# Filler weights of a scan: the low parts made by a ScalarE copy and an accumulating DMA

## Chip, core and metric

The kernel runs on one core of a Trainium2 chip. The metric is device time in microseconds of one execution, the median of several. The engines are named as in the profile: PE is TensorE's matmul and PEld its weight load, DVE is VectorE, ACT is ScalarE, POOL is GpSimd, SP is SyncE, which issues most of the DMAs.

## The reference, cut to what matters

One layer of a bidirectional encoder over 1024 positions and 1024 channels, all in float32:

```python
def _token_mixers(h, w_in, dw_w, dw_b, ln_w, ln_b, pw_w, lb, norm_w, o_w):
    proj = jnp.einsum("bsd,de->bse", h, w_in)
    glu_in, q, v, z_f, z_b, og, g_a, g_b = jnp.split(proj, SPLIT_POINTS, axis=-1)
    a = jax.nn.glu(glu_in, axis=-1)
    a = _dwconv_centred(a, dw_w, dw_b)
    a = jax.nn.silu(_layernorm(a, ln_w, ln_b))
    a = jnp.einsum("bsc,cd->bsd", a, pw_w)
    o = _bi_hgrn2(q, v, z_f, z_b, lb[0], lb[1])
    of = o * lax.rsqrt(jnp.mean(o * o, axis=-1, keepdims=True) + EPS)
    of = of.reshape(o.shape[0], o.shape[1], HGRN_WIDTH) * norm_w.astype(jnp.float32)
    bmix = (of * jax.nn.silu(og.astype(jnp.float32))).astype(h.dtype)
    bmix = jnp.einsum("bse,ed->bsd", bmix, o_w)
    return jax.nn.sigmoid(g_a) * a + jax.nn.sigmoid(g_b) * bmix
```

`_bi_hgrn2` is a chunkwise gated scan over 8 heads of 128 channels, once forward and once backward. After the mixers come an output projection with a residual, a gated feed-forward network and a final norm.

## The kernel before, in words

**Split products.** A float32 product is made of three matmuls of a faster 4-byte type (float32r). Each operand is split into a high part `hi`, a copy in that type, and a low part `lo`, the operand less `hi`. `mm3` (L142 to L149) issues, for one 128x128 block of weights, `hi` times the activation's high part (L147), `hi` times its low part (L148) and `lo` times its high part (L149). `split` (L122, its instructions on L123) makes the two parts: ACT copies, and DVE (or POOL) subtracts.

**Weight tiles.** A projection of 128 output channels over all positions is one job of `std_job` (L249). Its `prep` loads 128 columns of the weights (512 KB) into a raw page (tile `wr`, two buffers, L132, loaded by SP on L134) and splits it into two pages (tile `wp`, four buffers, L137). Its `run` goes through two halves of the positions with eight blocks each, 48 matmuls in all, and yields after every two blocks (a piece of six matmuls). `run_jobs` (L193) prepares the next job when a job starts, so that a tile's pages become free when the tile two before it is done. `Stream.fill(n)` runs n pieces.

**The stages.** The kernel first normalises the input, then projects, convolves, and goes on to the scan stage, which is about L1016 to L1417. Of the 56 column tiles for q, v, the gates and the forget gates, 34 are made as pairs in earlier stages. The other 22 (`rest`) are kept for the scan stage as filler: their stream is called `dense`. Twenty of them are one job each. The last two are one job (`duo_job`, L267) that alternates between two tiles.

**The scan stage.** There are 8 heads with two halves of 512 positions. For each half, `scan_inputs` (L1053) loads q and the forget gates (tile `zi`) and makes f and k on ACT, `scan_base` (L1077) prepares the factors `qF`, `kG`, `Qh`, `Kh` and `DE` on DVE (most through `tt`, L1042), and `scan_levels` (L1137) goes through four levels. In each, PE makes small matmuls (L1162, L1174, L1188) from qF and kG, and DVE then scales qF and kG for the next level. `scan_states` (L1238, PE on L1245 and L1254) and `scan_outputs` (L1277, PE on L1295, ACT on L1297, L1300 and L1314, POOL's `ors` on L509 and L510) follow. Between these steps `between` puts FILL = 1.3 pieces of `dense` on PE, and two steps of the next half's base on DVE. Ahead of the first head stand 21 pieces:

```python
    cur = Base(scan_inputs(0))
    ins = scan_inputs(1)
    dense.fill(21)
```

The order of PE's instructions is written out by hand (the order of the program). On the other engines a planner orders the instructions by a model of their times and by their place in the program, save those pinned to it.

**Accumulating DMAs.** Elsewhere in the kernel, sums of weight tiles are made by a DMA that POOL issues and that adds a tile in DRAM to a tile in SBUF (`G.dma_start(o, a, accum_op=ALU.add)`, L300, tile `sw` from `in_w_in_dram`). None is in the scan stage.

Of the kernel before, what the change touches and what calls it, by code (L numbers as in the profile page):

```python
# [10 lines left out]
F32 = mybir.dt.float32  # L11
# [3 lines left out]
AF = mybir.ActivationFunctionType  # L15
ALU = mybir.AluOpType
# [30 lines left out]
def tile_hybrid_encoder(  # L47
# [24 lines left out]
    V, A, G, T = nc.vector, nc.scalar, nc.gpsimd, nc.tensor  # L72

    S, D = x.shape[1], x.shape[2]
    ND = D // P
# [17 lines left out]
    def nm(s):  # L93
        uid[0] += 1
        return f"{s}_{uid[0]}"
# [3 lines left out]
    def bank(tag):  # L99
        return ps.tile([P, H], F32, tag=tag, name=nm(tag), bufs=BANKS[tag])  # L100

    def page(pool, tag, bufs, dt=F32):
        return pool.tile([P, H], dt, tag=tag, name=nm(tag), bufs=bufs)
# [18 lines left out]
    def split(hi, lo, src, eng, late=False):  # L122
        parts = A.copy(hi, src), eng.tensor_tensor(lo, src, hi.bitcast(F32), op=ALU.subtract)  # L123
        if late:
            for i in parts:
                pin(i)
        return hi, lo

    def w_cols(w, r0, nk, c0, cols=P):
        return w[0, r0 : r0 + nk * P, c0 : c0 + cols].rearrange("(k p) e -> p k e", p=P)  # L130

    def raw_w(src, nk):  # L132
        t = mp.tile([P, nk, P], F32, tag="wr", name=nm("wr"), bufs=2)
        nc.sync.dma_start(t, src)  # L134
        return t

    def w_page(nk, pool=None):  # L137
        if pool is None:
            return mp.tile([P, nk, P], F32R, tag="wp", name=nm("wp"), bufs=4)
        return pool.tile([P, nk, P], F32R, tag="wq", name=nm("wq"), bufs=3)  # L140

    def mm3(acc, w, act, k, first, last, again=False):  # L142


        whi, wlo = w
        ahi, alo = act
        T.matmul(acc, whi[:, k, :], ahi, start=first, stop=False, skip_group_check=again)  # L147
        T.matmul(acc, whi[:, k, :], alo, start=False, stop=False, skip_group_check=again)  # L148
        T.matmul(acc, wlo[:, k, :], ahi, start=False, stop=last, skip_group_check=again)  # L149
# [99 lines left out]
    def std_job(src, nk, acts, evac, halves=(0, 1), step=2):  # L249


        def prep():
            raw = raw_w(src, nk)
            return split(w_page(nk), w_page(nk), raw, V)

        def run(w, halves=halves):
            for half in halves:
                acc = bank("mm")
                for k in range(nk):
                    mm3(acc, w, acts(k, half), k, k == 0, k == nk - 1)  # L260
                    if k % step == step - 1 or k == nk - 1:
                        yield
                evac(half, acc)

        return prep, run

    def duo_job(src0, src1, nk, acts, evac0, evac1):  # L267

        both = [std_job(src0, nk, acts, evac0), std_job(src1, nk, acts, evac1)]

        def prep():
            return [p() for p, _ in both]

        def run(w):
            for half in range(2):
                for (_, r), wi in zip(both, w):
                    yield from r(wi, (half,))

        return prep, run
# [219 lines left out]
    def in_cols(c0):  # L499
        return w_cols(w_in, 0, ND, c0)  # L500
# [278 lines left out]
    def glu_tiles(j, halves):  # L779
        yield std_job(in_cols(CW + j * P), ND, h_std, evac_b(j), halves)  # L780
        yield std_job(in_cols(j * P), ND, h_std, evac_a(j), halves)
# [191 lines left out]
    for half in range(2):  # L973
# [27 lines left out]
        at = 0  # L1001
# [12 lines left out]


    rest = todo[2 * NPAIRS :]  # L1016
    rest_jobs = [std_job(in_cols(c), ND, h_std, e) for c, e in rest[:-2]]
    (c0, e0), (c1, e1) = rest[-2:]
    rest_jobs.append(duo_job(in_cols(c0), in_cols(c1), ND, h_std, e0, e1))

# [564 lines left out]
    def fetch(src):  # L1585
        t = page(fu, "ft", 8)
        nc.sync.dma_start(t, src)
        return t
# [211 lines left out]
```

## Time and profile before

| | us |
|---|---|
| Median of three runs | 1792.36 |
| Lowest and highest run | 1791.06, 1793.42 |
| Span of the profiled execution, first to last instruction | 1788.8 |
| PE busy in that span | 1733.0 |
| DVE busy | 1250.4 |
| ACT busy | 775.0 |
| POOL busy | 153.8 |

The profiled execution's own time is known as its span; the runs' times, which take in what lies around the span, were measured apart from it. A row of a group has the line, the engine, the operation, the tiles (output, then inputs), the shapes and the count; behind the bar are the busy time, the mean duration in ns and the idle time of the engine ahead of it with who ended it. A row in the order of time has its start, its length, and in brackets the idle time ahead of it with who ended that. A wait has who waited for whom, the total in us, the number of waits and the longest.

### The profile page before, as it was taken

How to read it: one execution, taken by the hardware profiler on the slowest of the kernel's cores; microseconds unless marked ns; L12 is line 12 of the kernel's file. 1: busy time of each engine (PE TensorE's matmuls, PEld its weight loads, DVE VectorE, ACT ScalarE, POOL GpSimd, SP SyncE). 2: the span in 40 equal slices, each digit the busy share in tenths (PEclk: the TensorE clock that was granted, in tenths of full speed). 3: DMA queues.
4: the chain of work that ended last, by engine and by line, in shares of the span. 5: the costliest groups of instructions: out<-in, count | busy, mean ns of one | idle time of the engine just before them, and what ended most of it. 6: DMA issues, size and time to landing. Idle time of an engine off the chain costs nothing.

```text
span 1788.8 us, 27583 instructions
## 1 busy us (share of the span) xinstructions
PE 1733.0 (97%) x10632; PEld 1416.7 (79%) x10638; DVE 1250.4 (70%) x1884; ACT 775.0 (43%) x1490; POOL 153.8 (9%) x168
## 2 busy tenths in 40 slices
PE   8989999999999999999999999999999999999997
PEld 6878877888777777777778888878888888888885
DVE  5599999746569999999645557667667667544455
ACT  7344333334555566655442245344344344422123
POOL 2201111000000000000000002011111111000000
PEclk9999999999999999999999999999999999999999
DMA  8657887743663433333257665567667665534233
GB/s 285 216 151 187 185 185 185 199 150 126 199 214 101 125 119 119 119 119 101 90 180 219 200 201 177 153 142 159 151 144 158 142 151 133 161 103 126 79 91 135
DMA packets 317705, 276.41 MB, mean 155 GB/s; under 512 B 14462, under 2 KB 242566, under 8 KB 317574
## 3 DMA queue, kind: packets, MB, share of 16 engines
q1 hardware_dynamic: 276406, 242.15, 43.1%
q0 software_dynamic: 41168, 32.51, 12.6%
q8 instruction: 83, 1.36, 0.3%
q14 instruction: 48, 0.39, 0.1%
HBM read 185.73 MB, written 72.61 MB: 144 GB/s over the span
## 4 chain that ended last, share of the span: by engine, by line
PE 65%; DVE 19%; DMA 5%; issue 4%; ACT 4%; POOL 1%; SPq 0%; POOLq 0%; DVEq 0%; ACTq 0%
PE mm L147 16%; PE mm L148 16%; PE mm L149 16%; PE sc L147 3%; PE sc L149 3%; PE sc L148 3%; DVE acc L955 2%; DVE kG L1042 2%; DVE DE L1042 2%; DVE qF L1042 2%; DVE wp L123 2%; PE tr L147 1%; PE tr L149 1%; PE tr L148 1%; DVE DE L1098 1%
## 5 line engine op out<-in xcount | busy, mean ns | idle before, releaser
L147 PE MATMUL mm<-hx,wp 128*128 128x512 f32 x1128 | 454.8, 403 | 9.8 <-DVE ev L717 4.3
L149 PE MATMUL mm<-hx,wp 128*128 128x512 f32 x1128 | 441.7, 392 | 1.9 <-DVE wp L123 1.9
L148 PE MATMUL mm<-hx,wp 128*128 128x512 f32 x1128 | 441.4, 391 | 0.0
L123 ACT CAST wp<-wr 128x1024 fp32r<-128x1024 f32 (+2 forms) x179 | 167.0, 934 | 359.6 <-PE mm L148 271.5
L147 PEld LDWEIGHTS mm<-hx,wp 128*128 128x128 f32 x1128 | 212.5, 188 | 55.7 <-DVE ev L717 6.7
L123 DVE TENSOR_TENSOR wp<-wr,wp 128x1024 fp32r<-128x1024 f32 (+2 forms) x177 | 191.4, 1082 | 90.4 <-ACT wp L123 90.1
L149 PEld LDWEIGHTS mm<-hx,wp 128*128 128x128 f32 x1128 | 212.6, 188 | 49.3 <-DVE wp L123 3.2
L148 PEld LDWEIGHTS mm<-hx,wp 128*128 128x128 f32 x1128 | 212.9, 189 | 40.4 <-issue 0.2
L955 DVE SCALAR_TENSOR_TENSOR acc<-gl,v_b,acc 128x1024 f32<-128x1024 f32 x120 | 149.0, 1277 | 0.5
L1651 DVE TENSOR_TENSOR xr<-mm,xr 128x512 f32<-128x512 f32 x48 | 33.2, 691 | 73.1 <-PE mm L149 73.1
L367 ACT COPY su<-mm 128x512 f32<-128x512 f32 x78 | 45.2, 579 | 62.5 <-PE mm L149 61.5
L123 ACT CAST wq<-sw 128x1024 fp32r<-128x1024 f32 x39 | 41.0, 1051 | 64.4 <-issue 28.6
L1500 DVE SCALAR_TENSOR_TENSOR tm<-gp,v_a,tm 128x512 f32<-128x512 f32 x88 | 65.9, 749 | 2.0
L147 PE MATMUL mm<-hy,wp 128*128 128x512 f32 x156 | 61.5, 394 | 1.4 <-ACT su L367 1.4
L148 PE MATMUL mm<-hy,wp 128*128 128x512 f32 x156 | 61.1, 392 | 0.0
L147 PE MATMUL sc<-hy,wq 128*128 128x512 f32 x156 | 61.1, 392 | 0.0
L149 PE MATMUL sc<-hy,wq 128*128 128x512 f32 x156 | 61.1, 391 | 0.0
L147 PE MATMUL tr<-hx,wp 128*128 128x512 f32 x156 | 60.8, 390 | 0.0
L149 PE MATMUL tr<-hx,wp 128*128 128x512 f32 x156 | 60.7, 389 | 0.0
L148 PE MATMUL tr<-hx,wp 128*128 128x512 f32 x156 | 60.7, 389 | 0.0
L148 PE MATMUL sc<-hy,wq 128*128 128x512 f32 x156 | 60.7, 389 | 0.0
L149 PE MATMUL mm<-hy,wp 128*128 128x512 f32 x156 | 60.6, 389 | 0.0
(368 smaller groups left out, 3467.6 us busy)
## 6 DMA issues: line engine op xcount, KB each, us to landing
wr<-in_w_in_dram SPq DMA_DIRECT2D x56, 512.0 KB, 4.7
wr<-in_ffn_w_up_dram SPq DMA_DIRECT2D x24, 512.0 KB, 4.9
sw<-in_ffn_w_up_dram SPq DMA_DIRECT2D x44, 256.0 KB, 3.0
d_g<-ft SPq DMA_DIRECT2D x44, 256.0 KB, 2.7
sw<-in_ffn_w_up_dram POOLq DMA_DIRECT2D x20, 512.0 KB, 8.3
sw<-in_w_in_dram SPq DMA_DIRECT2D x34, 256.0 KB, 3.2
d_z<-ev SPq DMA_DIRECT2D x32, 256.0 KB, 3.1
zi<-d_z SPq DMA_DIRECT2D x32, 256.0 KB, 3.2
```

The source lines that it names most:

```text
L123: parts = A.copy(hi, src), eng.tensor_tensor(lo, src, hi.bitcast(F32), op=ALU.subtract)
L147: T.matmul(acc, whi[:, k, :], ahi, start=first, stop=False, skip_group_check=again)
L148: T.matmul(acc, whi[:, k, :], alo, start=False, stop=False, skip_group_check=again)
L149: T.matmul(acc, wlo[:, k, :], ahi, start=False, stop=last, skip_group_check=again)
L367: A.copy(t, acc)
L955: V.scalar_tensor_tensor(acc, g[:, k : k + S], tap(k), acc, op0=ALU.mult, op1=ALU.add)
L1042: V.tensor_tensor(o, a, b, op=op)
L1098: V.reciprocal(ed(D, 7), ed(0, D + 7))
L1500: V.scalar_tensor_tensor(c, g[:, o + k : o + k + H], vec("fdw", k * NF + j), c, op0=ALU.mult, op1=ALU.add,)
L1651: V.tensor_tensor(xr[i][half], acc, xr[i][half], op=ALU.add)
```

## The change

For twenty of the twenty-two filler tiles (all but the closing pair) the low part is made in another way. ACT still copies the raw page into `hi`. Then ACT, not DVE, writes minus `hi` into `lo`, and POOL issues a DMA that adds the weights in DRAM to `lo`, a second read of the same 512 KB. The raw page is then read by ACT alone. Besides, each job's `prep` asks for the raw page of the job after it, before its own copies; `fetch` remembers pages by their place in the weights.

```diff
+    def dma_job(src, nk, acts, evac, fetch, after):
+        def prep():
+            raw = fetch(src)
+            if after is not None:
+                fetch(after)
+            hi, lo = w_page(nk), w_page(nk)
+            A.copy(hi, raw)
+            A.activation(lo, hi.bitcast(F32), AF.Copy, scale=-1.0)
+            G.dma_start(lo, src, accum_op=ALU.add)
+            return hi, lo
+
+        return prep, std_job(None, nk, acts, evac)[1]
...
     rest = todo[2 * NPAIRS :]
-    rest_jobs = [std_job(in_cols(c), ND, h_std, e) for c, e in rest[:-2]]
+    fetched = {}
+
+    def fetch(src):
+        at = src.offset
+        if at not in fetched:
+            fetched[at] = raw_w(src, ND)
+        return fetched[at]
+
+    srcs = [in_cols(c) for c, _ in rest[:-2]]
+    rest_jobs = [
+        dma_job(src, ND, h_std, e, fetch, after)
+        for src, (_, e), after in zip(srcs, rest, srcs[1:] + [None])
+    ]
     (c0, e0), (c1, e1) = rest[-2:]
     rest_jobs.append(duo_job(in_cols(c0), in_cols(c1), ND, h_std, e0, e1))
```

## The prediction

> **What bounds the kernel now.** I read the page first, then the busy time by stretch, the waits and the chain of the stretch that the change touches, and last the order of time around the first filler tiles.
>
> ```profile
> span 1788.8 us, 27583 instructions
> PE 1733.0 (97%) x10632; PEld 1416.7 (79%) x10638; DVE 1250.4 (70%) x1884; ACT 775.0 (43%) x1490; POOL 153.8 (9%) x168
> ```
>
> TensorE bounds the whole. The edit works only in the scan stage, whose matmul tiles fill TensorE between the scan's steps, so the stretch table matters more.
>
> ```profile
> 495.00:520.00 25.00, 25.00 (x111) 20.59 (x110) 11.92 (x19) 15.38 (x23) 1.31 (x4) 1.00 0.81 255
> 525.00:866.00 341.00, 322.71 (x4210) 263.90 (x4215) 316.85 (x645) 197.67 (x482) 11.88 (x12) 1.00 0.35 111
> ```
>
> The columns are start:end, length, then the busy time of PE, PEld, DVE, ACT and POOL, the granted clock, the DMA share and GB/s. At the entry, 495 to 520, PE is busy in all 25.00 us and DVE in 11.92: PE alone sets the time there. In the body, 525 to 866, DVE is busy in 316.85 of 341 us (93%), PE has 18.3 us idle, ACT stands at 58%, and the clock is full.
>
> ```profile
> PE ob L1162 <- DVE qF L1042: 6.0, 7, 1.5
> PE tr L1245 <- DVE kG L1042: 4.7, 6, 1.8
> PE sc L1188 <- DVE qF L1042: 3.2, 6, 1.2
> PE ob L1295 <- DVE D L1230: 1.1, 1, 1.1
> PE ob L1162 <- ACT wp L123: 0.9, 1, 0.9
> DVE f L1074 <- ACT f L1067: 9.8, 4, 4.0
> DVE wp L123 <- ACT wp L123: 7.7, 4, 3.3
> ```
>
> These waits of the body (total us, times, longest) say whom PE waits for: DVE, 6.0 + 4.7 + 3.2 + 1.1 = 15.0 us in twenty waits. One of them in the order of time:
>
> ```profile
> 597.97 1.21 DVE L123 TENSOR_TENSOR wp<-wr,wp 128x1024 fp32r<-128x1024 f32 x1
> 599.10 0.68 DVE L1042 TENSOR_TENSOR qF<-qF,tb 128x512 f32<-128x512 f32 x1
> 599.93 0.46 PE L1162 MATMUL ob<-qF,A 128*32 128x32 f32 x32 [0.92 <-DVE qF L1042]
> ```
>
> The low part of a filler tile (L123, 1.21 us) stands on DVE ahead of the scan's qF, and PE idles 0.92 us for that qF. This is the place where the change can win.
>
> **What the body gains.** The chain of work of 525 to 866:
>
> ```profile
> by line: DVE kG L1042 11.1%; DVE qF L1042 10.1%; DVE DE L1042 9.7%; DVE wp L123 4.7%; DVE DE L1098 4.6%; DVE Kh L1045 4.6%; DVE Qh L1042 4.1%; issue 4.0%; DVE Sb L1347 3.0%; ACT tm L1314 2.7%; ACT jk L1300 2.5%; DVE Sf L1262 2.2%; ACT f L10
> 526.04 1.13 DVE wp L123
> 864.46 1.14 DVE wp L123
> ```
>
> DVE wp is 4.7% of 341 us, 16.0 us: fourteen steps of some 1.14 us, of which the first and the last stand here. The change takes twenty of the twenty-two low parts off DVE; the closing pair of tiles keeps its own. The step at 864.46 belongs to the pair and stays. The one at 526.04 lies before PE has reached the scan's first level, so its removal frees nothing on PE. Twelve steps are left: 12 x 1.14 = 13.7 us. The bound from above is what PE waits for DVE, 15.0. The bound from below is zero, if DVE then waits elsewhere as long (the f and wp rows: 9.8 + 7.7 us of DVE idle are no DVE work at all). I take 13.7, nearer to the upper end, because those twelve steps lie on the chain, not merely on a busy engine. What is late next is PE itself, at 95% of the body.
>
> **What ACT and the queues pay.**
>
> ```profile
> L123 ACT CAST wp<-wr 128x1024 fp32r<-128x1024 f32 x21 | 21.9, 1044 | 15.0 <-PE mm L148 12.8 <-DMA wr<-in_w_in_dram 2.1
> L123 DVE TENSOR_TENSOR wp<-wr,wp 128x1024 fp32r<-128x1024 f32 x21 | 25.7, 1222 | 12.7 <-ACT wp L123 12.7
> L300 POOL DMA_DIRECT2D sw<-in_w_in_dram x11: 1570/1579/1764, 122.5 to 316.7; - x11
> POOL ors L509 <- ACT jk L1300: 354.9, 7, 87.2
> q0 software_dynamic: 41168, 32.51, 12.6%
> ```
>
> The scaled copy reads and writes 1024 columns as the cast does, so I price it at the cast's 1.044 us: 20 x 1.044 = 20.9 us more on ACT against 20 x 1.222 = 24.4 us less on DVE. ACT's own steps on the chain (tm 2.7% and jk 2.5% in the row above, a further one cut off by the row's end) are some 7%, and 7% of 20.9 is 1.5 us. From below it is zero, where ACT idles behind the cast; from above three times the 0.9 us that PE already waits for an ACT cast, 2.7 us. I take 1.5. Queued behind the new copy on ACT are the scan's A, f, kT and tm, and it is for these that DVE and PE wait.
>
> POOL gets 20 issues of 1.579 us, 31.6 us in a stretch with 11.88 us of work. In the body only the ors pairs stand in its queue (seven, long idle before them); an ors caught behind an issue waits up to 1.6 us for it. The issues fill 9% of the stretch, so of seven ors 0.6 would be caught, for half an issue each: 0.5 us at most on the chain, and zero in the sum. What is new on POOL is that it waits for ACT's copy: behind that wait stand the next ors, and behind them ACT's tm. The accumulating traffic is 20 x 0.524 = 10.5 MB; at the q0 row's rate (12.6% of 1788.8 us for 32.51 MB) that is 73 us of all sixteen engines, and lifts the body's share from 0.35 to 0.56. I cost it at nothing, since the scan's own loads are issued far ahead of their use, as this pair of rows shows for zi (15.7 us from issue to first use):
>
> ```profile
> 612.16 2.07 SPq L1063 DMA_DIRECT2D zi<-d_z  x2
> 627.82 0.63 ACT L1064 ACTIVATE k<-zi 128x512 f32<-128x512 f32 x1
> ```
>
> Without that cover each load that meets a new transfer would be late by that transfer's share of the engines, 73 / 20 = 3.6 us.
>
> The raw loads issued two tiles ahead change nothing:
>
> ```profile
> 559.36 0.38 SPq L134 DMA_DIRECT2D wr<-in_w_in_dram  x1
> 596.32 1.04 ACT L123 CAST wp<-wr 128x1024 fp32r<-128x1024 f32 x1
> ```
>
> SP issues this tile's load 37 us before its cast already now, so the wait that an earlier issue could take away isn't there. On SP's queue the load moves ahead of a few stores and zi loads, at 0.38 us of issue each: zero, from both sides, as long as zi keeps its 15.7 us.
>
> **What the entry loses.** The new low part is hi, then the negative copy, then POOL's issue, then the landing, and the third product of the first tile needs it.
>
> ```profile
> 497.75 1.05 ACT L123 CAST wp<-wr 128x1024 fp32r<-128x1024 f32 x1 [1.68 <-PE mm L148]
> 498.84 1.22 DVE L123 TENSOR_TENSOR wp<-wr,wp 128x1024 fp32r<-128x1024 f32 x1 [2.52 <-ACT wp L123]
> 500.58 0.39 PE L147 MATMUL mm<-hx,wp 128*128 128x512 f32 x1
> 501.03 0.40 PE L149 MATMUL mm<-hx,wp 128*128 128x512 f32 x1
> sw<-in_w_in_dram POOLq DMA_DIRECT2D x11, 512.0 KB, 8.8
> DMA to landing us min/median/max: 3.2/4.2/10.7
> wr<-in_w_in_dram SPq DMA_DIRECT2D x21, 512.0 KB, 4.6
> 501.27 0.21 POOL L1037 MEMSET dg<- 128x128 f32 x1
> 529.25 0.73 PE L1174 MATMUL sc<-Qh,Kh 128*32 128x32 f32 x62
> ```
>
> The cast waits for a page that PE frees at about 497.7 (its releaser is PE), so it can't start earlier. It ends at 498.80, the negative copy at 499.84, and the accumulating DMA lands T later. The eleven accumulating loads of the same 512 KB from the same tensor land in 8.8 us (issue time included), so T = 8.8: 508.64. PE wants it at 501.03 (L149), and its order is fixed by hand: **a stall of 7.6 us**, where PE has been without a gap. PE reaches the scan's first level (L1174, 529.25) by working through the filler, so that the level moves by the whole stall. In general T - 1.2. The bounds for T: 4.6, the plain load of the same size, and 10.7, the longest landing of that line; if POOL's memsets (the last at 501.27) come first, 1.6 more.
>
> The second tile has its pages at 500.7 and a whole tile of time. The third must wait until the first is done:
>
> ```profile
> 511.25 0.39 PE L149 MATMUL mm<-hx,wp 128*128 128x512 f32 x1
> 522.81 0.39 PE L149 MATMUL mm<-hx,wp 128*128 128x512 f32 x1
> 524.42 1.04 ACT L123 CAST wp<-wr 128x1024 fp32r<-128x1024 f32 x1
> 539.81 0.39 PE L149 MATMUL mm<-hx,wp 128*128 128x512 f32 x1
> ```
>
> The first tile ends at 511.64; plus cast, copy and T that is 511.64 + 1.05 + 1.04 + 8.8 = 522.5 against a need at 522.81, both pushed by the same stall: no loss at 8.8, T - 9.1 above that. From the fourth on there are 15.4 us from cast to need (524.42 to 539.81, the shortest of the body) against 2.1 + T = 10.9, so the landing is hidden; it would show from T = 13.3.
>
> **The sum**, against this execution: -13.7 + 1.5 + 7.6 = -4.6 us on the span of 1788.8. The three runs' median, 1792.36, lies 3.6 above the span and within 0.1% of its fellows; I carry the difference over: 1792.36 - 4.6 = **1787.8**.
>
> By the Trainium skill, page "DMA: Bandwidth & Descriptors", section "Anatomy of one DMA — SWDGE (gpsimd) path", a GpSimd-issued DMA costs about 2.0 us plus bytes / 436 GB/s: 3.2 us for 512 KB, an estimate. With it the stall is 2.0 and the sum -10.2, 1782.2. The trace speaks against it for an accumulating transfer: 8.8.
>
> **Rivals.** About 0.2%, 3.6 us, is what a measurement of this kernel tells from no change.
>
> Slower: the landing at the entry. The entry is the stretch with a DMA share of 0.81, two accumulating transfers overlap there, and no DMA of the trace writes into an fp32r tile, so T may be longer than anything shown. Both the first and the third tile pay: (T - 1.2) + (T - 9.1) - 12.2. That is nothing at T = 11.2, 3.6 slower from T = 13.0, and 7.5 slower at 15: 1799.9. Against it: the eleven transfers behind the 8.8 and 10.7 ran in a stretch as busy as this one.
>
> ```profile
> 200.00:300.00 100.00, 98.94 (x434) 80.95 (x433) 97.22 (x93) 37.29 (x54) 16.66 (x15) 1.00 0.81 185
> ```
>
> There the share was 0.81 too. Chance 0.18.
>
> No change: DVE's saving turns into DVE idling. A run of DVE begins when ACT delivers f (9.8 us in four waits), and ACT gets the extra copy; the waits of DVE for a cast (7.7 us) show that a low part sometimes stood where DVE had nothing else. If half the twelve steps pay, -6.9 + 1.5 + 7.6 = +2.2: 1794.6. From 5.5 to 12.7 us of gain it is within 3.6. Chance 0.22, with 0.06 more for T between 11 and 13 with the full gain. Below 5.5 it is slower: 0.11.
>
> Faster by more: the accumulate lands like a plain load, T = 4.6, the stall is 3.4 and the sum -8.8: 1783.6. For it: both move the same 512 KB in 512-byte rows. Against it: the 8.8 row. Chance 0.05, the page's rule included.
>
> **How the numbers follow.** The forecast itself has 0.38. Faster: 0.38 + 0.05 = 0.43. Same: 0.22 + 0.06 = 0.28. Slower: 0.18 + 0.11 = 0.29. The range runs from the upper bound of the gain with the short landing, -15.0 + 3.4 + 1.5 = -10.1, rounded out to 1781, to the long landing of 15 us, 1800. The forecast's own range, T from 7 to 10.7 and the gain from 12.7 to 15.0, is 1785 to 1791.
>
> **What would show it.** Right: the low part's DVE rows are down to the closing pair in the scan; twenty ACT copies near 1.04 us; twenty POOL issues near 1.58 us that land in about 8.8; a gap of 7 to 8 us on PE before L149 near 501, and the scan's first L1174 that much after 529.25; behind it, PE's waits for DVE in the body down from 15.0 to below 3, and the body itself some 12 us shorter. Wrong: landings over 13 us or a second gap at the third tile (the entry loses more); PE waits for DVE still above 8 with longer DVE waits for ACT's f (the body gains less); PE waiting for low parts past the third tile, where I cost nothing.

## The result, and the profile after

| | before | after |
|---|---|---|
| Median of six runs, us | 1793.24 | 1802.58 |
| Lowest and highest, us | 1791.06, 1794.90 | 1798.58, 1808.42 |
| Ratio to before, 95% interval | | 1.0048 [1.0027, 1.0069] |
| Span of the profiled execution, us | 1788.8 | 1796.8 (its own time 1798.58) |

The change makes the kernel slower by about 0.5%, 8.6 us. The forecast was 1787.8 in a range of 1781 to 1800. One run of the kernel before took 3062.93 us and is left out of the highest and of the ratio; the median of the other five is 1793.07.

Lines of the changed kernel are 27 higher behind the edit: L1201 is the old L1174, L1272 the old L1245. The page's first lines, and the windows of the entry and the body, the body's moved on by 12.7 us as the scan's first level is:

```profile
span 1796.8 us, 27634 instructions
PE 1736.9 (97%) x10638; PEld 1417.6 (79%) x10638; DVE 1230.1 (68%) x1864; ACT 792.5 (44%) x1510; POOL 187.1 (10%) x188
```

```profile
500.00:505.00 5.00, 0.19 (x1) 0.00 (x0) 0.00 (x0) 3.77 (x4) 3.72 (x6) 0.78 0.98 252
505.00:510.00 5.00, 0.00 (x0) 0.00 (x0) 0.00 (x0) 0.63 (x1) 0.21 (x1) 0.50 1.27 264
510.00:515.00 5.00, 4.28 (x10) 3.41 (x11) 1.11 (x3) 3.60 (x6) 0.00 (x0) 0.50 1.27 231
515.00:520.00 5.00, 5.00 (x20) 4.01 (x20) 4.16 (x6) 1.28 (x3) 0.00 (x0) 0.86 0.67 235
537.70:878.70 341.00, 327.71 (x4241) 267.57 (x4240) 298.18 (x621) 211.88 (x506) 41.94 (x31) 1.00 0.57 138
```

DVE is busy 20 us less and ACT 17.5 more, as the change wants. But at the entry PE stands still through 505 to 510, and the granted clock, 1.00 here in the kernel before, falls to 0.50 and comes back only between 515 and 520. In the body PE's idle time fell from 18.3 to 13.3 us (341 less the busy time) while DVE's busy time fell by 18.7.

I split the span at three events that every kernel here has: the first matmul of the filler (L147 with `hx`), the first L1174 of the scan, and the first L1174 of its sixteenth half. The **entry** is from the first to the second, the **body** from the second to the third.

| | before | after | difference |
|---|---|---|---|
| Entry, us | 28.67 | 42.38 | +13.7 |
| Body, us | 346.76 | 341.52 | -5.2 |

The two together give +8.5, against 8.0 by the spans and 8.6 by the ratio. The entry in the order of time, POOL and then PE:

```profile
499.58 1.62 POOL L277 DMA_DIRECT2D wp<-in_w_in_dram  x1 [44.04 <-PE mm L148]
503.63 1.59 POOL L277 DMA_DIRECT2D wp<-in_w_in_dram  x1 [1.28 <-ACT wp L276]
```

```profile
499.80 0.40 PE L148 MATMUL mm<-hx,wp 128*128 128x512 f32 x1
510.72 0.79 PE L149 MATMUL mm<-hx,wp 128*128 128x512 f32 x1 [10.53 <-DMA wp<-in_w_in_dram]
511.31 0.63 PE L147 MATMUL mm<-hx,wp 128*128 128x512 f32 x1
...
516.01 0.58 PE L149 MATMUL mm<-hx,wp 128*128 128x512 f32 x1
516.42 0.39 PE L147 MATMUL mm<-hx,wp 128*128 128x512 f32 x1
...
541.95 0.73 PE L1201 MATMUL sc<-Qh,Kh 128*32 128x32 f32 x62
```

POOL issues the first accumulating DMA at 499.58 and PE's L149 runs at 510.72: the landing took 11.1 us. The next matmul should have begun 0.23 us behind the L148; it began 10.7 us later than that. Then thirteen matmuls, to 516.42, follow each other at some 0.43 us (rows of 0.63) instead of 0.23 (rows of 0.39): 5.7 us for what takes 3.0, another 2.7. Together that is 13.4 of the entry's 13.7.

### The profile page after: what moved, and what is told of

Same layout as the page of the kernel before. It is cut to its first block, busy times and chain, and to the rows that moved or that the text cites. A ratio compares the mean times of both kernels' runs of the same rounds, so it can differ in the third digit from the quotient of the medians.

```text
span 1796.8 us, 27634 instructions
## 1 busy us (share of the span) xinstructions
PE 1736.9 (97%) x10638; PEld 1417.6 (79%) x10638; DVE 1230.1 (68%) x1864; ACT 792.5 (44%) x1510; POOL 187.1 (10%) x188
## 3 DMA queue, kind: packets, MB, share of 16 engines
q0 software_dynamic: 61968, 43.00, 17.5%
## 4 chain that ended last, share of the span: by engine, by line
PE 64%; DVE 18%; DMA 9%; issue 5%; ACT 3%; POOL 0%; SPq 0%; POOLq 0%; DVEq 0%; ACTq 0%
PE mm L147 16%; PE mm L149 16%; PE mm L148 16%; DVE acc L970 4%; PE sc L149 3%; PE sc L147 3%; PE sc L148 3%; DVE qF L1069 2%; DVE kG L1069 2%; DMA sw<-in_w_in_dram 2%; DVE DE L1069 2%; DMA wr<-wr 2%; DMA sw<-in_ffn_w_up_dram 2%; DVE wp L123 1%; PE tr L147 1%
## 5 line engine op out<-in xcount | busy, mean ns | idle before, releaser
L147 PE MATMUL mm<-hx,wp 128*128 128x512 f32 x1128 | 455.5, 404 | 9.6 <-DVE ev L732 5.2
L149 PE MATMUL mm<-hx,wp 128*128 128x512 f32 x1128 | 443.4, 393 | 12.2 <-DMA wp<-in_w_in_dram 10.5
L148 PE MATMUL mm<-hx,wp 128*128 128x512 f32 x1128 | 442.1, 392 | 0.0
L123 ACT CAST wp<-wr 128x1024 fp32r<-128x1024 f32 (+2 forms) x159 | 146.2, 920 | 373.3 <-PE mm L148 215.7
L149 PEld LDWEIGHTS mm<-hx,wp 128*128 128x128 f32 x1128 | 213.1, 189 | 61.5 <-DMA wp<-in_w_in_dram 11.3
L147 PEld LDWEIGHTS mm<-hx,wp 128*128 128x128 f32 x1128 | 213.2, 189 | 55.9 <-DVE ev L732 7.8
L148 PEld LDWEIGHTS mm<-hx,wp 128*128 128x128 f32 x1128 | 213.3, 189 | 40.3 <-issue 0.2
L123 DVE TENSOR_TENSOR wp<-wr,wp 128x1024 fp32r<-128x1024 f32 (+2 forms) x157 | 167.1, 1065 | 106.6 <-ACT wp L123 106.2
L315 POOL DMA_DIRECT2D wr<-sw x31 | 27.7, 894 | 374.0 <-DVE wp L123 163.6
L382 ACT COPY su<-mm 128x512 f32<-128x512 f32 x78 | 45.1, 578 | 40.6 <-PE mm L149 39.5
L147 PE MATMUL mm<-hy,wp 128*128 128x512 f32 x156 | 61.5, 394 | 1.4 <-ACT su L382 1.4
L148 PE MATMUL mm<-hy,wp 128*128 128x512 f32 x156 | 61.2, 392 | 0.0
L147 PE MATMUL sc<-hy,wq 128*128 128x512 f32 x156 | 61.1, 392 | 0.0
L149 PE MATMUL sc<-hy,wq 128*128 128x512 f32 x156 | 61.0, 391 | 0.0
L147 PE MATMUL tr<-hx,wp 128*128 128x512 f32 x156 | 60.8, 390 | 0.0
L149 PE MATMUL tr<-hx,wp 128*128 128x512 f32 x156 | 60.7, 389 | 0.0
L148 PE MATMUL tr<-hx,wp 128*128 128x512 f32 x156 | 60.7, 389 | 0.0
L148 PE MATMUL sc<-hy,wq 128*128 128x512 f32 x156 | 60.7, 389 | 0.0
```

Of the source, the lines that this page charges most:

```text
L382: A.copy(t, acc)
```

## The experiments

The change and the ten kernels first, with their ratio to the kernel before, and the entry and body of their profiled execution as differences to that of before. The ratio's us are the ratio's distance from 1 times 1793. In experiment 2 the entry is counted from the first of the added matmuls.

| kernel | ratio, 95% interval | as us | entry | body | entry + body |
|---|---|---|---|---|---|
| the change | 1.0048 [1.0027, 1.0069] | +8.6 | +13.7 | -5.2 | +8.5 |
| 1 first three tiles on DVE | 0.9973 [0.9961, 0.9985] | -4.8 | 0.0 | -4.0 | -4.0 |
| 2 PE kept busy | 1.0090 [1.0076, 1.0105] | +16.1 | +21.9 | -4.3 | +17.6 |
| 3 no low parts | 0.9960 [0.9947, 0.9973] | -7.2 | 0.0 | -5.4 | -5.4 |
| 4 no accumulating DMA | 0.9981 [0.9971, 0.9991] | -3.4 | 0.0 | -3.5 | -3.5 |
| 5 as 1, kG first on DVE | 0.9966 [0.9952, 0.9979] | -6.1 | 0.0 | -5.9 | -5.9 |
| 6 second and third tile on DVE | 1.0044 [1.0028, 1.0060] | +7.9 | +13.2 | -3.7 | +9.5 |
| 7 raw load not ahead | 1.0055 [1.0036, 1.0075] | +9.9 | +13.3 | -5.2 | +8.1 |
| 8 first tile on DVE | 1.0015 [1.0005, 1.0026] | +2.7 | +8.3 | -5.0 | +3.3 |
| 9 order alone, low parts on DVE | 0.9999 [0.9990, 1.0008] | -0.2 | 0.0 | -0.5 | -0.5 |
| 10 late scan loads | 1.0069 [1.0055, 1.0083] | +12.4 | +17.5 | -5.1 | +12.4 |

The two segments add up to the ratio's difference within 2 us in every row, so the question splits in two: why the entry loses 13.7 and why the body gains only 5. The ratios come from several runs, the segments from one execution each, and single executions differ: outside the two segments by up to 4.5 us (experiment 1's span is 1789.3), and in the body, among the seven kernels that treat it alike (the change and 1, 2, 6, 7, 8 and 10), from 341.5 to 343.1 us. A difference of 1.5 us between two bodies is therefore not read here.

**1. The first three tiles on DVE.**

```diff
-        dma_job(src, ND, h_std, e, fetch, after)
+        std_job(src, ND, h_std, e) if n < 3 else dma_job(src, ND, h_std, e, fetch, after)
...
```

> The first three filler tiles are split on DVE as before, the other seventeen by the copy and the accumulating DMA. Theory (entry by the first tile's landing alone, 10.5 us of PE idle plus some 2.9 us of half clock): the gap before L149 is gone, the clock stays at 1.00, and from the first filler matmul to the first L1174 it takes 28.7 us as before, not 42.4; the body, from the first to the last half of the scan, keeps 341.5 us against 346.8; time some 5 us under the kernel before, ratio 0.997. Rival (the entry suffers from the added DMA traffic or the raw loads moved ahead): the entry stays above 32 us and the ratio at 1.000 or more.

The entry is 28.68 us, that of the kernel before, with PE without a gap and the clock at 1.00 up to the scan's first level. The body keeps a gain of 4.0 us, and the kernel is faster than before. The loss of the change lies in its first three tiles alone.

**2. PE kept busy at the entry.**

```diff
+        run = std_job(None, nk, acts, evac)[1]
+        def warm(w):
+            spare = bank("ob")
+            for n in range(44):
+                T.matmul(spare, w[0][:, n % nk, :], acts(n % nk, 0)[0], start=True, stop=True)
+            yield from run(w)
-        return prep, std_job(None, nk, acts, evac)[1]
+        return prep, warm if src.offset == srcs[0].offset else run
```

> The change as it is, but PE runs 44 matmuls into a spare bank (10.1 us, results unused) ahead of the first filler tile, while that tile's low part is under way. Theory (the half clock is the follow of PE's idling): the first L149 comes at the same distance behind its low part's issue, 11 us, the granted clock stays at 1.00 there, and the entry takes some 39.5 us against 42.4; time 3 us under the change. Rival (the clock fell for another reason, or its cost is hidden by the scan's own start): the entry stays at 42 us.

The gap at the first tile is gone and the clock stays at 1.00 there, but the time is higher, not lower. The rows of ACT, and then of PE, tell why:

```profile
530.84 1.16 ACT L1099 ACTIVATE k<-zi 128x512 f32<-128x512 f32 x2 [4.71 <-DVE Kh L1080]
...
534.82 1.05 ACT L275 CAST wp<-wr 128x1024 fp32r<-128x1024 f32 x1
```

```profile
545.57 0.80 PE L149 MATMUL mm<-hx,wp 128*128 128x512 f32 x1 [8.55 <-DMA wp<-in_w_in_dram]
```

PE now idles 8.55 us for the **third** tile. Its cast stands on ACT behind the scan's k, which waits 4.71 us for a page that DVE has to free, and the clock falls to half for 10.24 us after that. So the theory's mechanism holds, the half clock follows PE's idling, but the idling moved to another tile. In the changed kernel the same cast began at 523.90, as soon as the first tile was done, and the third tile shows no gap. Without the third tile's 8.55 us and the half clock behind it the entry would be some 39 us, near the 39.5 expected (50.6 less 8.55 and an estimated 2.8); that is worked out, not measured.

**3. No low parts at all** (for tiles 4 to 20 the high part is used in the low part's place; first three as in 1).

```diff
-            A.activation(lo, hi.bitcast(F32), AF.Copy, scale=-1.0)
-            G.dma_start(lo, src, accum_op=ALU.add)
-            return hi, lo
+            G.memset(lo.bitcast(F32)[:, 0, 0:1], 0.0)
+            return hi, hi
...
```

> As e1, but the low parts of tiles four to twenty are left out: no subtraction, no negative copy, no DMA, and the third product takes the high part again, so that PE's work is the same (the output is not the reference's). Theory (DVE's saved time turns into DVE waiting for PE at the end of a half, because its queue holds the next half's work ahead of the level's kG): the body stays at 340 to 342 us, 1787 to 1789. Rival (the gain is there but ACT's copies and the DMA traffic eat it): the body falls to 335 or less and the time to 1782.

**4. No accumulating DMA** (the low part is minus `hi` alone; first three as in 1).

```diff
-            G.dma_start(lo, src, accum_op=ALU.add)
...
```

> As e1, with the negative copies on ACT but without the accumulating DMAs of tiles four to twenty (the low part is then minus the high part; the output is not the reference's). Theory: the body as in e1 and e3, 340 to 342 us. Rival (DMA traffic costs): body like e3's low value, below e1 by 3 us or more. Rival (ACT's copies cost): like e1, but above e3 by 3 us or more.

With no ACT copy, no POOL issue and no second read of the weights, the body gains 5.4 us; with all of them it gains 4.0 in experiment 1 and 5.2 in the change. Without the DMA traffic alone it gains 3.5, not more than with it. So the traffic shows no cost, and ACT's copies and POOL cost at most about 2 us (3 against 1 and against 4), which these runs can't tell from nothing. They don't eat what DVE saves: the 18.7 us of DVE work were worth 3.5 to 5.4 us to begin with.

**5. kG first on DVE** (first three as in 1). The base work of the half after the next is held on DVE's queue behind the last scaling of kG of the half at hand.

```diff
+            if h == 64:
+                last_kg.append(kg.ins)
...
+            held = last_kg[-1] if last_kg else None
...
             def between(fill):
                 dense.fill(fill)
-                if ahead is not None:
+                if ahead is not None and held is not None:
+                    with tc.issue_after(held):
+                        ahead.step(BASE_STEPS)
+                elif ahead is not None:
                     ahead.step(BASE_STEPS)
```

> The first three filler tiles are split on DVE as before, the other seventeen by the accumulating DMA, and the base work of the half after the next is held back in the program so that DVE has the present half's last scaling of kG ahead of it. Theory (order on DVE's queue: in the changed kernel PE's waits for kG, 6.3 us in eight, come from base steps of 1 to 2 us that stand ahead of it): these waits fall below 2 us, the body from first to last L1174 falls from 342.7 to 338-339 us, and the time is some 4 us below that of the kernel with the first three tiles on DVE, a ratio of about 0.995 to the kernel before. Rival (what is left of PE's waits is the way from PE through DVE and back, and base steps that are held back are late for the next half): the kG waits turn into waits for qF, Qh or Sf, body 342 to 345, ratio 0.997 to 0.999.

The reason for it is this piece of the changed kernel, DVE and then PE:

```profile
690.01 1.76 DVE L1125 RECIPROCAL DE<-DE 128x256 f32<-128x256 f32 x1
691.68 0.63 DVE L1069 TENSOR_TENSOR kG<-kG,tb 128x512 f32<-128x512 f32 x1
692.36 0.66 PE L1272 MATMUL tr<-ident,kG 128*128 128x128 f32 x4 [1.74 <-DVE kG L1069]
```

A reciprocal for a later half stands ahead of the kG that PE waits for: the same pattern that the low part showed before at 597.97, with another step in its place. With the new order, PE's waits in the body (525 to 866; L1189, L1274, L1215 and L1324 are the old L1162, L1245, L1188 and L1295):

```profile
PE ob L1189 <- DVE qF L1069: 3.9, 7, 1.3
PE tr L1274 <- DVE kG L1240: 2.4, 6, 0.8
PE sc L1215 <- DVE qF L1069: 2.1, 3, 1.3
PE ob L1324 <- DVE tb L1069: 1.3, 1, 1.3
PE ob L1324 <- DVE D L1259: 1.3, 3, 0.5
```

The waits for kG fall from 6.5 us (experiment 1) to 2.4, where below 2 was expected, but those for qF rise from 4.5 to 6.0, as the rival had it. The body is 340.84 us against 342.72, 1.9 shorter where some 4 were expected, and only 0.7 shorter than that of the change. The order moves PE's waits; that it shortens the body is hardly more than the spread of single executions. The ratio, 0.9966, is the best of all kernels here that do the whole computation; its interval overlaps that of experiment 1, so it is not shown that the order takes anything off that kernel's time.

**6. Only the second and the third tile on DVE.**

```diff
...
+        std_job(src, ND, h_std, e) if n in (1, 2) else dma_job(src, ND, h_std, e, fetch, after)
...
```

> Only the second and the third filler tile are split on DVE, the first and the other seventeen by the accumulating DMA, so that one accumulating transfer is under way at the entry and not two. Theory A (the second accumulate, issued 4 us after the first, slows the first one's landing): it lands after about 8.8 us in place of 11.1, PE's gap ahead of the first L149 falls from 10.5 to about 8, and the entry from 42.4 to about 40 us. Theory B (a single transfer takes as long in this place): gap 10 to 11 us, entry 41.5 to 42.5. By both, the clock stays at half speed for a while behind the gap, and the third tile shows no gap. Time some 3 to 6 us over the kernel before by A, 7 to 9 by B.

POOL and PE at the first tile:

```profile
501.25 1.62 POOL L277 DMA_DIRECT2D wp<-in_w_in_dram  x1 [43.92 <-ACT wp L276]
...
512.89 0.79 PE L149 MATMUL mm<-hx,wp 128*128 128x512 f32 x1 [10.99 <-DMA wp<-in_w_in_dram]
```

A single accumulating transfer took 11.6 us, the gap is 10.99 and the entry 41.89: theory B. The second accumulate is not what made the first one late. The body is the longest of the seven, 343.07 us: behind a gap of 1.84 us that PE spent waiting for kG, the clock fell to half for 3.41 us at 694.6.

**7. Raw load not asked ahead.**

```diff
-            if after is not None:
-                fetch(after)
```

> As the changed kernel, but no job asks for the raw page of the job after it: raw loads stand where they stood before. Theory (the prediction's: that part changes nothing): entry 42.4 +- 1 us, body 341.5 +- 1.5, the same time as the changed kernel within 3 us. Rival (the raw load asked ahead crowds the transfers at the entry and makes the first accumulate late): gap at the first L149 falls from 10.5 to 8-9 us, entry to 40. A third way (the planner orders ACT or DVE otherwise): body differs by more than 2 us either way.

The gap is 10.17 us, the entry 41.95 and the body 341.55 against 42.38 and 341.52. The third tile shows a gap of 0.88 us here; its accumulate took 9.6 us to land. The part of the change that asks for raw pages ahead shows no worth either way, as predicted.

**8. Only the first tile on DVE.**

```diff
...
+        std_job(src, ND, h_std, e) if n < 1 else dma_job(src, ND, h_std, e, fetch, after)
...
```

> Only the first filler tile is split on DVE, the other nineteen by the accumulating DMA. Theory (only the very first low part has no cover; the second tile's DMA is issued at about 503.6 and lands at 11 us, 514.7, against a need at about 512.5; third tile: first tile's end 511.6 plus cast, copy and 11 us is 524.9 against 522.8): two gaps of 2 to 3 us each, no half clock as they are too short, entry 28.7 + 4 to 5 = 33 us, time about that of the kernel before. Rival (landings of 7.9 us, the median of this kernel's twenty): no gap, entry 28.7, ratio 0.997 as with the first three tiles on DVE. Other rival (third tile's casts queued late on ACT behind the scan's k, as in the kernel whose first gap was filled with dummy matmuls): a gap of 6 to 9 us at the third tile with half clock behind it, entry 38 to 40, about 5 us slower than before.

POOL and PE at the second tile:

```profile
507.43 1.62 POOL L277 DMA_DIRECT2D wp<-in_w_in_dram  x1 [2.65 <-ACT wp L276]
...
521.29 0.79 PE L149 MATMUL mm<-hx,wp 128*128 128x512 f32 x1 [5.88 <-DMA wp<-in_w_in_dram]
521.88 0.63 PE L147 MATMUL mm<-hx,wp 128*128 128x512 f32 x1
```

One gap of 5.88 us where two of 2 to 3 were expected. The first filler matmul runs at 503.88 here, so the DMA was issued 3.6 us behind it, about where the expectation had it; it landed after 13.9 us where 11 were expected, the longest landing of all here, and that is 2.8 us of the miss. The clock fell to half for 6.83 us after a gap of this length too. The third tile, pushed back, showed no gap. So the first two tiles' low parts lack cover, and the third's has hardly any: it shows a gap in experiments 2, 7 and 10.

**9. The order alone,** the edit of 5 in the kernel before.

> The kernel before, all low parts on DVE, with only the order of the previous experiment: the base work of the half after the next is held behind the present half's last scaling of kG on DVE. Theory A (the low parts taken off DVE and the order help each other: with 16 us more work on DVE, base work that is held back comes late and PE waits for qF and Qh instead): body 345 to 348 us, ratio 0.998 to 1.002. Theory B (the order alone makes the gain and the change adds next to nothing): PE's waits for kG fall from 4.9 to about 2 us, body 343 to 345, ratio about 0.997, the same as with the accumulating DMA.

PE's waits in 525 to 866 (L1247 is the old L1245):

```profile
PE ob L1162 <- DVE qF L1042: 8.3, 9, 2.0
PE sc L1188 <- DVE qF L1042: 2.5, 4, 1.3
PE tr L1247 <- DVE kG L1213: 2.3, 3, 0.9
```

The waits for kG fall from 4.7 to 2.3 us while those for qF rise from 9.2 to 10.8: no gain, ratio 0.9999. The profiled execution also had 3.41 us of half clock at 536. This is as theory A has it, in which base work that is held back comes late while DVE still has the low parts to do. That reason is argued, not tested; and since the gain by the order in experiment 5 isn't shown either, the two need not help each other.

**10. The scan's loads late.** q and zi of the second half and og of the first head are queued on SP behind a raw load. The expectation calls it the fourth tile's; it is the fifth's, since each job asks for the page of the next: SP issued it at 527.62 and the first of the held loads at 528.68.

```diff
...
+        raws.append(nc.sync.dma_start(t, src))
...
-    ins = scan_inputs(1)
-    dense.fill(21)
+    dense.fill(17); hold.append(raws[-1].ins)
+    with tc.issue_after(hold[0]): ins = scan_inputs(1)
+    dense.fill(4)
...
+            with tc.issue_after(hold[0]): nc.sync.dma_start(gates[half], d_og[h][half])
...
```

> The changed kernel, with the scan's loads of the second half (q, zi) and of the first head's og moved on SP's queue behind the fourth filler tile's raw load, so that 1.25 MB less is loaded while the first accumulating DMAs are under way. Theory (the first accumulate lands late, 11.1 us for 8.8, because the scan's loads share the sixteen engines, whose share is 1.2 there): the gap ahead of the first L149 falls from 10.5 to 8-9 us and the entry from 42.4 to about 40. Rival (the landing is slow by itself at this place): gap 10 to 11.5 us, entry 42 to 43. The body may pay for late loads: PE or ACT waits for zi at the second half, some us.

PE at the first and at the third tile, whose accumulates POOL issued at 503.34 and 529.32:

```profile
513.73 0.79 PE L149 MATMUL mm<-hx,wp 128*128 128x512 f32 x1 [9.93 <-DMA wp<-in_w_in_dram]
...
541.13 0.50 PE L149 MATMUL mm<-hx,wp 128*128 128x512 f32 x1 [3.07 <-DMA wp<-in_w_in_dram]
```

The landing takes 10.4 us and not 11.1. But the experiment did not do what it was made for: in the 11 us from the issue on, the other queues still moved 2.18 MB (2.15 in the changed kernel), since raw loads filled the place of those held back (0.87 MB in packets of 512 bytes against 0.51). So it doesn't tell its two theories apart. The held loads moved into the third tile's stretch: its accumulate took 11.8 us to land, PE idled 3.07 us there, and the entry grew to 46.13.

## Why the prediction was wrong

**The entry's mechanism and its place were right; two terms of it were wrong.** The gap stands at the first L149, as predicted, and the scan's first level moves by all of it. The landing was put at 8.8 us, the median of the eleven accumulating loads of before, and measured 11.1, 2.3 us more; POOL issued it 0.7 us later against the first matmul than the working had it. Some 0.4 of that is a bank that ACT evacuated between the cast and the negative copy, and 0.3 passes between the copy's end and POOL's issue:

```profile
496.79 1.05 ACT L275 CAST wp<-wr 128x1024 fp32r<-128x1024 f32 x1 [1.71 <-PE mm L148]
497.74 0.58 ACT L737 COPY ev<-mm 128x512 f32<-128x512 f32 x1
498.22 1.06 ACT L276 ACTIVATE wp<-wp 128x1024 fp32r<-128x1024 f32 x1
```

With these the gap is 10.7 and not 7.6. The changed kernel's own twenty landings show that 8.8 was fair for a typical one and wrong for this place:

```profile
wp<-in_w_in_dram POOLq DMA_DIRECT2D x20, 512.0 KB, 7.9
...
DMA to landing us min/median/max: 6.9/7.9/13.0
```

Least, median and largest landing: the largest is the second tile's, and the first tile's, 11.1, is the next. In the trace of the changed kernel, landings grow with what the other queues move in the 8 us behind the issue: four with under 0.8 MB took 6.6 to 7.5 us to the last packet, three with over 1.35 MB 9.0 to 10.0. That is a reading over the seventeen landings from the fourth tile on (correlation 0.65; in the traces of experiments 1, 2, 5, 6, 7, 8 and 10 it is 0.25 to 0.72). In the five kernels whose first tile has an accumulate (the change, 2, 6, 7 and 10) its landing took 9.6 to 11.6 us, always more than 8.8; experiment 6 shows that it is not the second accumulate, and experiment 10 did not test the rest. The prediction held the stretch of the eleven loads of before to be as busy as the entry; the DMA engines' share was 0.87 to 1.01 during those landings and 1.10 during this one. Some landings of the body at 1.06 to 1.11 took 9.3 to 10.3 us, so the share alone does not give 11.1. Why the landing is slow at the entry stays open.

**The clock was left out altogether.** An idle PE was priced at its idle time. The trace shows that it costs more: 2.6 us into the gap the granted clock fell to 0.50, stayed there for 13.65 us, and PE lost another 2.7 us after the data had come. Gaps of 5.9 to 11 us all did this (experiments 2, 6, 7, 8 and 10 too), the half clock lasting 6.83, 10.24 or 13.65 us, multiples of 3.41. The kernel before had no such stretch between the first filler matmul and the sixteenth half; it had 3.41 us at 311, as much at 1168, and 8.79 at its end. The Trainium skill, page "TensorE: Matmul & The Clock Gate", section "Part 1: The HAM clock gate", states the rule: the clock is halved after at least one idle window of about 3.4 us and given back after about as much work. The traces agree in part: the stretches come in pieces of that length, and full speed came 3.6 to 6.0 us after PE's restart from the long gaps. But the drop came 2.6 to 5.0 us into those gaps, and gaps shorter than a window had one too (1.84 us in experiment 6), so here the measurement decides. A stall predicted at 7.6 us should have carried this term.

**The body's gain was mis-sized: 13.7 less 1.5 predicted, 5.2 measured.** The step that failed is "those twelve steps lie on the chain, not merely on a busy engine". The prediction read DVE wp's 4.7% of the chain of waits as time that comes back. The same row of the changed kernel, for its own 341 us, shows what took the place:

```profile
by line: DVE qF L1069 9.7%; DVE kG L1069 9.2%; DVE DE L1069 8.6%; PE mm L147 5.7%; PE mm L148 5.2%; PE mm L149 5.2%; DVE DE L1125 4.6%; PE ob L1322 4.5%; DVE Kh L1072 4.0%; DVE Qh L1069 3.9%; DVE Sb L1374 3.9%; issue 2.6%; PE tr L1272 2.0%;
```

DVE wp is gone from it, and the filler's matmuls, no group of which reached 2.2% before, now hold 16.1%. Where DVE was freed, the next thing late was PE's own work in its fixed order, behind which DVE then waits. The prediction names this ("What is late next is PE itself"), but its sum has no term for it. PE's waits and DVE's, in 537.7 to 878.7:

```profile
PE tr L1272 <- DVE kG L1069: 6.3, 8, 1.7
PE ob L1189 <- DVE qF L1069: 2.3, 6, 0.5
PE ob L1322 <- DVE tb L1069: 1.7, 1, 1.7
PE ob L1322 <- DVE D L1257: 1.3, 3, 0.5
PE sc L1215 <- DVE qF L1069: 1.3, 1, 1.3
```

```profile
DVE Sf L1287 <- PE ob L1281: 22.3, 6, 4.6
DVE qF L1069 <- PE sc L1189: 7.1, 4, 6.4
DVE f L1101 <- ACT f L1094: 3.0, 3, 1.6
```

PE still waits 12.9 us for DVE (15.0 before; "below 3" was predicted, and above 8 was named as the sign of being wrong). DVE's waits for PE's `ob` and `sc` grew to 29.4 us, from 4.0 in the body before. So DVE's saving turned into DVE idling, the rival of "no change", but by another engine than it named: not ACT's f, whose wait fell from 9.8 to 3.0, but PE. Experiment 3 shows that the gain isn't eaten by what was put in the step's place: with no low-part work at all from the fourth tile on the body gains 5.4. That PE's fixed order is what takes the rest is read from the chain and the waits; no run here changes that order. The example that the prediction generalised from (0.92 us of PE's idle behind a low part) was a true one; of the seventeen low parts that the change takes off DVE between 525 and 850, six had a gap of PE (over 0.2 us) within 5 us of their start in the trace of before, and these gaps come to 3.7 us. That is far nearer to the 5.2 that was measured than 13.7 is. But the 5 us were chosen after the result: 3 us would give 2.0, and 8 us 5.6.

**ACT's price was read from a row cut at its end.** The prediction put ACT at some 7% of the body's chain. Summed over the whole chain of that stretch ACT holds 16.4%, which by the same rule would be 3.4 us and not 1.5. The experiments put the cost at no more than about 2, so the misreading did not decide the result.

**Right:** the new steps on ACT and POOL take the times predicted:

```profile
L276 ACT ACTIVATE wp<-wp x20: 1044/1061/1082, 498.2 to 852.2; 128x1024 fp32r<-128x1024 f32 x20
L277 POOL DMA_DIRECT2D wp<-in_w_in_dram x20: 1540/1556/1890, 499.6 to 853.6; - x20
```

The DMA share in the body is 0.57 (0.56 predicted) and shows no cost (experiment 4). The landings from the fourth tile on are hidden: in no kernel here does PE wait for one. The raw loads asked ahead show no effect (experiment 7). **Right by a narrow margin:** the third tile. By the prediction's T - 9.1 it costs nothing up to T = 9.1, and its landing took 8.6 us: 535.33, with PE's L149 at 535.38. Where it took 9.6 and 11.8 us (experiments 7 and 10), the formula gives 0.5 and 2.7 us, and the gaps were 0.88 and 3.07. It leaves out that ACT's queue can be late: in experiment 2 the landing took 7.9 us and the gap was 8.55.

In the sum: entry 13.7 for 7.6 (gap 3.1, clock 2.7, 0.3 unaccounted) and body -5.2 for -12.2, that is 6.1 + 7.0 = 13.1 of the 14.8 us between the forecast and the median. The rest comes from carrying one execution over to the median: the forecast added 3.6 us to the span, and the median after lies 5.8 above its span, since the profiled execution was the fastest of the six; the segments also exceed the difference of the spans by 0.5.

## What to carry to other kernels

A step's share of the chain of waits is not what its removal brings: here 16 us on the chain were worth 5, because the next engine was nearly as late. Pricing the removal by each wait of the bounding engine that has the step close ahead of it would have come nearer; that is hindsight from one kernel. An asynchronous step in place of a synchronous one needs cover at the first use, where a stream starts: leave the first tiles on the old way, which here turned 0.5% slower into 0.3% faster. A stall of TensorE of some 6 us or more had half clock behind it every time here; in the changed kernel that was 2.7 us on top.

## What the runs showed of the hardware

A packet of 512 bytes of the accumulating DMA kept its engine busy for 68 ns on average in the scan stage, one of a plain load of the same size 30 ns (from the packets' records). The half clock also followed shorter gaps: 3.41 us of it behind the 3.07 us of experiment 10, behind 1.96 us in experiment 9, and behind 1.84 us in experiment 6; two gaps of 1.7 us in the changed kernel's body had none. What these drops share is a thin stretch: in the 3.41 us before each drop between 300 and 1200 us, in the traces of before, the change and experiments 1, 2 and 6 to 10, PE was busy in 54% at most. The first packet of an accumulating transfer left as early as 2.3 us after the issue in the body, and 3.6 to 5.4 us after it for the first one of the entry. With these, landings of the same 512 KB took from 6.9 to 13.9 us. The Trainium skill, page "DMA: Bandwidth & Descriptors", section "Anatomy of one DMA — SWDGE (gpsimd) path", would give 3.2 us, an estimate from its fit; every landing here was at least twice that.
